# Attention gate's second block and the forget gate's 16 columns as two blocks of 264 columns

## Chip, cores and metric

The kernel runs on one core of one Trainium2 chip. The metric is the device time of one execution in microseconds, as the median of several. Its engines are TensorE (PE, with its weight loads as PEld), VectorE (DVE), ScalarE (ACT), GpSimd (POOL) and SyncE (SP), each with an instruction order of its own; DMA transfers are issued from SP's queue (loads) and POOL's (stores).

## What is computed

Two layers of a trunk over 512 tokens of 2048 features, in float32. Each layer normalizes the tokens, multiplies them with one wide matrix, cuts the result by columns, and runs two groups of heads on it:

```python
def hybrid_layer(x, w_in, w_out, g_pre, g_post, w_alpha, b_alpha, g_gla, g_att, rel_bias):
    h = rmsnorm(x, g_pre)
    z = h @ w_in
    gq, gk, gv, gg, ga, aq, ak, av, ag = split_columns(z)
    log_a = jax.nn.log_sigmoid((ga @ w_alpha + b_alpha).astype(jnp.float32)) / GLA_TAU
    o_gla = gla_chunk_causal(gq, gk, gv, log_a)
    o_gla = rmsnorm(o_gla, g_gla) * jax.nn.silu(gg)
    o_att = chunk_band_attention(aq, ak, av, rel_bias)
    o_att = rmsnorm(o_att, g_att) * jax.nn.silu(ag)
    y = jnp.concatenate([o_gla, o_att], axis=-1) @ w_out
    return x + rmsnorm(y, g_post)
```

The change is about two of the pieces of `z`: `ag`, 1024 columns, the gate of the attention heads, and `ga`, only 16 columns, the low-rank input of the forget gate `log_a`.

## The kernel before

**Precision.** A float32 operand is kept as a high part, which TensorE's fp32r format holds, and a low part, the rest. A product is three matmuls: high x high, high x low, low x high. For a block of weights the high part `wh` is a cast on ACT (L201) and the low part `wl` a subtraction on DVE (L210); for sums of tokens the same pair stands at L105 and L106.

**Blocks.** The columns of `w_in` come in blocks of 512. Each block is loaded in eight chunks of 256 features (128 partitions x 2 x 512, 512 KB). A list `stream` of jobs, one for each chunk, fixes the order of all loads, casts and subtractions; `ahead` runs up to five loads, four casts and three subtractions in front of the matmuls. The rings that the jobs use have 5 buffers for `raw` (the loaded chunk), 4 for `wh`, 3 for `wl`.

**Two kinds of products.** Most blocks are taken in pairs by `fast_gemm` (L324 on), which computes four quarter products with seven multiplications, as Strassen does; its matmuls are at L388 (512 columns) and L378 (256 columns). It needs sums and differences S1 to S4 of the token operands. The two blocks AG0 and AG1 of the attention gate are plain products in `std_gemm`, with the matmul at L310: for each chunk and each tile of 128 tokens 2 x 3 matmuls of 512 columns, into one PSUM tile for each of the token tiles. `lag` holds back the last chunks, which are then taken token tile by token tile, so that the tiles are complete one after another. `gate` (L730 on) puts a SiLU over a finished tile (L733) and stores it.

**What else is going on in these stages.** `pump` takes steps of side tasks between the matmuls, at a `rate` for each group of them. In layer 0, AG0 runs on the raw tokens; meanwhile `first_operands` makes the normalized token operands `a`, `g`, `sa` (multiplications L659 and splits L105 and L106 on DVE and ACT), which AG1 needs, chunk by chunk. In layer 1 the gate blocks run twice, for the first and the second half of the tokens, with a transposition of the normalized tokens (L521) and its evictions (L532) in between. `token_sums` makes S1 to S4 in both layers (L570 to L579 on DVE, then L105 and L106), in a few slots g4 to g7 and g10 that are used again and again, and POOL's queue stores them to memory (`S<-g`). So the cast that fills a slot anew waits for the store before. Then the pair AV of `fast_gemm` begins.

**The forget gate.** `load_forget_gate` loads the 16 columns of `w_ga` apart from the blocks, splits them with six small casts and subtractions, and lays them out as 96 columns (three groups of high and low part). The task `forget_gate` multiplies all token operands with them: 64 matmuls a layer at L752, with weights of 96 columns over 256 tokens, spread among AG1's matmuls. A copy (L759), a cast (L760) and a subtraction (L761) make the transposed `gaT` from it, which is stored for later use.

**The order** in each engine's queue is that of a scheduler, which moves instructions that do not depend on each other; rates, lags and rings decide what it can move.

## Time and profile before

| What | Value |
|---|---|
| Median of 3 runs (lowest, highest) | 1615.99 us (1614.28, 1617.05) |
| Span of the profiled execution | 1613.3 us |
| PE matmuls in the profile | 8938 |
| Layer 0's gate blocks: AG1 from, AV from | 50.65 us, 101.98 us |
| Layer 1's gate blocks: from, AV from | 804.93 us, 903.91 us |
| Granted TensorE clock | 1.00 in the stages of the gate blocks |

The profile is one execution, and its span can be compared with spans only; the runs' median is 2.7 us above it. The time of a matmul in the lists of single instructions runs from its start to its modelled end and overlaps that of the next one; its price in a stream is the distance from start to start, which the chain of work gives as length by count. The same holds in part for DVE, where an instruction of 0.68 us can be followed by the next one after 0.60.

### The profile page before, as it was taken

To read this page: it belongs to the slowest core of one execution; us is meant where nothing else is said; L and a number is where in the kernel's file an instruction comes from. 1 tells how busy PE (TensorE), PEld (TensorE's weight loads), DVE (VectorE), ACT (ScalarE), POOL (GpSimd) and SP (SyncE) were. 2 spreads that over 40 slices of the span, in tenths; PEclk is the share of its full clock that TensorE was granted. 3 is DMA by queue.
4 is the path that set the end of the run, shared out by engine and by line. 5 is a ranking of instruction groups with operands and counts; after the bars stand their busy time and mean duration, and the time that the engine had idled before them with its cause. 6 is when DMAs were issued, how large, how long until landed. Compare 5 with 4: busy or idle time off the path is not lost.

```text
span 1613.3 us, 24483 instructions
## 1 busy us (share of the span) xinstructions
PE 1600.6 (99%) x8938; PEld 1372.9 (85%) x8938; DVE 1271.7 (79%) x1646; ACT 919.5 (57%) x1509; POOL 127.5 (8%) x192
## 2 busy tenths in 40 slices
PE   9999999999999999999999999999999999999997
PEld 7888999998888778888888889999988887788886
DVE  5977777678677878998998677776786878689887
ACT  7544445657555546565796444455675545566654
POOL 0120000010000010100122000000100100101001
PEclk9999999999999999999999999999999999999999
DMA  9797686785868768689779786857858687686986
GB/s 371 258 371 271 238 304 206 230 308 168 286 213 282 261 221 313 227 309 377 270 267 369 312 312 222 306 193 260 299 198 292 209 301 254 221 307 228 342 302 190
DMA packets 133928, 438.17 MB, mean 272 GB/s; under 512 B 14404, under 2 KB 27204, under 8 KB 133776
## 3 DMA queue, kind: packets, MB, share of 16 engines
q1 hardware_dynamic: 117072, 375.99, 67.2%
q0 software_dynamic: 16160, 59.53, 10.0%
q8 instruction: 71, 1.16, 0.3%
q10 hardware_dynamic: 576, 1.08, 0.2%
q14 instruction: 49, 0.40, 0.1%
HBM read 377.02 MB, written 61.62 MB: 272 GB/s over the span
## 4 chain that ended last, share of the span: by engine, by line
PE 95%; DVE 2%; DMA 1%; ACT 1%; issue 1%; DVEq 0%; SPq 0%; ACTq 0%
PE mm L388 54%; PE mm L378 19%; PE mm L310 10%; PE ax L945 2%; PE ax L388 2%; PE ax L1131 1%; PE ax L928 1%; PE ax L752 1%; PE ax L1103 1%; PE ax L908 1%; PE ax L907 1%; PE ax L906 1%; DVE wl L210 1%; DMA bias<-in_rel_dram 0%; PE ax L1223 0%
## 5 line engine op out<-in xcount | busy, mean ns | idle before, releaser
L388 PE MATMUL mm<-wh,sa 128*128 128x512 f32 x1600 | 517.7, 394 | 0.6 <-ACT wh L201 0.5
L201 ACT CAST wh<-H 128x1024 fp32r<-128x1024 f32 x256 | 268.5, 1051 | 213.9 <-PE mm L388 94.0
L210 DVE TENSOR_TENSOR wl<-H,wh 128x1024 fp32r<-128x1024 f32 x256 | 311.6, 1219 | 94.3 <-PE mm L388 33.0
L388 PEld LDWEIGHTS mm<-wh,sa 128*128 128x128 f32 x1600 | 299.4, 188 | 72.8 <-issue 8.8
L201 ACT CAST wh<-raw 128x1024 fp32r<-128x1024 f32 (+1 forms) x233 | 244.0, 1051 | 197.1 <-PE mm L388 91.2
L210 DVE TENSOR_TENSOR wl<-raw,wh 128x1024 fp32r<-128x1024 f32 (+1 forms) x233 | 282.0, 1213 | 58.1 <-PE mm L388 25.7
L388 PE MATMUL mm<-wl,sa 128*128 128x512 f32 x800 | 312.6, 391 | 0.0
L378 PE MATMUL mm<-sa,wh 128*128 128x256 f32 x1280 | 237.4, 285 | 0.0
L388 PE MATMUL mm<-wh,a 128*128 128x512 f32 x640 | 211.5, 394 | 0.0
L378 PEld LDWEIGHTS mm<-sa,wh 128*128 128x128 f32 x1280 | 200.3, 191 | 0.3
L378 PE MATMUL mm<-sa,wl 128*128 128x256 f32 x640 | 180.9, 283 | 0.0
L388 PEld LDWEIGHTS mm<-wl,sa 128*128 128x128 f32 x800 | 150.3, 188 | 30.0 <-DVE wl L210 0.4
L195 DVE TENSOR_TENSOR H<-H,raw 128x1024 f32<-128x1024 f32 x144 | 174.6, 1217 | 1.0
L388 PEld LDWEIGHTS mm<-wh,a 128*128 128x128 f32 x640 | 119.5, 188 | 24.9
L388 PE MATMUL mm<-wl,a 128*128 128x512 f32 x320 | 125.6, 393 | 0.0
L378 PEld LDWEIGHTS mm<-sa,wl 128*128 128x128 f32 x640 | 122.5, 191 | 0.0
L430 POOL TENSOR_TENSOR sm<-sm,mhalf 128x2 f32<-128x2 f32 (+2 forms) x40 | 51.4, 1285 | 761.2 <-DVE sm L955 456.3
L197 DVE TENSOR_TENSOR raw<-H,raw 128x1024 f32<-128x1024 f32 x56 | 68.5, 1222 | 51.8 <-DMA raw<-in_w_dram 51.4
L388 PE MATMUL mm<-wh,g 128*128 128x512 f32 x320 | 101.5, 391 | 0.0
L378 PE MATMUL mm<-a,wh 128*128 128x256 f32 x512 | 95.4, 285 | 0.0
L340 ACT COPY ev<-mm 128x512 f32<-128x512 f32 x104 | 60.9, 585 | 60.5 <-PE mm L388 43.8
L216 DVE TENSOR_TENSOR H<-H,raw 128x1024 f32<-128x1024 f32 x48 | 58.7, 1223 | 35.3 <-DMA raw<-in_w_dram 35.0
(250 smaller groups left out, 2323.6 us busy)
## 6 DMA issues: line engine op xcount, KB each, us to landing
raw<-in_w_dram SPq DMA_DIRECT2D x311, 512.0 KB, 5.1
sa<-S SPq DMA_DIRECT2D x184, 512.0 KB, 4.5
H<-in_w_dram SPq DMA_DIRECT2D x64, 512.0 KB, 5.2
sa<-A SPq DMA_DIRECT2D x48, 512.0 KB, 5.8
S<-g POOLq DMA_DIRECT2D x32, 512.0 KB, 9.1
sa<-oS SPq DMA_DIRECT2D x32, 512.0 KB, 5.2
oS<-g POOLq DMA_DIRECT2D x16, 512.0 KB, 4.4
oS<-sa POOLq DMA_DIRECT2D x16, 512.0 KB, 5.7
```

Of the source, the lines that this page charges most:

```text
L195: nc.vector.tensor_tensor(out=h, in0=h, in1=r, op=ALU.add)
L197: nc.vector.tensor_tensor(out=r, in0=h, in1=r, op=ALU.subtract)
L201: last_cast[0] = nc.scalar.copy(self.wh[:, z, :], src[:, z, :]).ins
L210: last_low[0] = nc.vector.tensor_tensor(out=self.wl[:, z, :], in0=self.src[:, z, :], in1=self.wh[:, z, :].bitcast(F32), op=ALU.subtract).ins
L216: nc.vector.tensor_tensor(out=h, in0=h, in1=self.src, op=ALU.add)
L310: nc.tensor.matmul(pss[o], a(part, kk, o) if callable(a) else a[:, part, t], rhs[:, kk, :], start=(i == 0 and kk == 0 and m == 0), stop=(i ...
L340: last_copy[0] = nc.scalar.copy(e, src[t]).ins
L378: nc.tensor.matmul(dst, lhs[:, kk, f], a[:, part, tok], start=(fresh and kk == 0 and m == 0 and ft % 2 == 0), stop=(c == 3 and kk == 1 and ...
L388: last_mm[0] = nc.tensor.matmul(out_ps[t], a[:, part, tok], rhs[:, kk, :], start=(fresh and kk == 0 and m == 0), stop=(c == 3 and kk == 1 ...
L430: nc.gpsimd.tensor_tensor(out=out_r, in0=v, in1=mhalf[:, : v.shape[-1]], op=ALU.pow)
L752: nc.tensor.matmul(ps[0:96, half * 256 : (half + 1) * 256], wga[kt // 10][:, kt % 10, :], op[:, i, (kt % 2) * 256 : (kt % 2 + 1) * 256], s ...
L945: nc.tensor.matmul(o, self.pt[i][:, j * P : (j + 1) * P], av[hd // 4, j // 2][:, j % 2, (hd % 4) * P : (hd % 4 + 1) * P], start=(j == 0), ...
```

## The change

AG1 keeps only its first 264 columns. A third block AG2 takes the remaining 248 columns of the attention gate and the 16 columns `ga`, so that it is 264 wide as well. Both come from a new array `w_ag`, with chunks of 128 x 2 x 264 (264 KB). Jobs, tiles of PSUM and the SiLU use the first 264 (or 248) columns of their tiles. In layer 0 the rate of the side tasks goes from 1.8 to 1.0 and the lag from 2 to 1 in AG1, 2 in AG2; in layer 1 the rate is 1.3 in AG0 and 0.7 in AG1 and AG2.

```diff
+        def cut(self, tile_):
+            if self.b0 not in (AG1, AG2):
+                return tile_
+            return tile_.rearrange("p k n -> p (k n)")[:, : 2 * N1].rearrange("p (k n) -> p k n", k=2)
...
+            if blk in (AG1, AG2):
+                last_load[0] = nc.sync.dma_start(flat(tile_)[:, : 2 * N1], w_ag[self.l, int(blk == AG2), c]).ins
+                return self.cut(tile_)
...
-            stream += [Job(l, "std", c, b) for half in range(2) for b in (AG0, AG1) for c in CO]
+            stream += [Job(l, "std", c, b) for half in range(2) for b in (AG0, AG1, AG2) for c in CO]
...
-        pss = {o: ps_mm.tile([P, W], F32, tag="mm", name=nm("mm")) for o in outs}
+        wide = W if blk == AG0 else N1
+        pss = {o: ps_mm.tile([P, W], F32, tag="mm", name=nm("mm"))[:, :wide] for o in outs}
...
-            std_gemm(l, AG1, range(NT), CO, operand_in, gate_evac(1), rate=1.8, lag=2)
+            std_gemm(l, AG1, range(NT), CO, operand_in, gate_evac(1), rate=1.0, lag=1)
+            std_gemm(l, AG2, range(NT), CO, operand_in, gate_evac(2), rate=1.0, lag=2)
...
-                        l, b, (2 * half, 2 * half + 1), CO, operand_in, gate_evac(q), rate=1.3, lag=2 * half * q,
+                        l, b, (2 * half, 2 * half + 1), CO, operand_in, gate_evac(q), rate=0.7 if q else 1.3,
+                        lag=2 * half * (q // 2),
```

When a tile of AG2 is complete, DVE copies its last 16 columns three times into a slot `ga` of zeros (new line 752). The forget gate's own load, casts, subtractions and 64 matmuls a layer are gone; four transposes a layer (new line 764) turn `ga` into the same 96 rows. The task starts after the gate blocks and runs in AV, which now pumps at a rate of 0.5.

```diff
         def gate_evac(q):
             def f(o, ps):
                 gate(q, o, ps)
+                if q == 2:
+                    if not ga:
+                        ga.append(slot("g16", [NT, 3, 2, GA]))
+                        nc.gpsimd.memset(ga[0][:, :, :, 1, :], 0.0)
+                    for g in range(3):
+                        nc.vector.tensor_copy(ga[0][:, o, g, 0, :], ps[:, N1 - GA :])
             return f
...
-            for half in range(2):
-                for k in range(2 * KT):
-                    kt, i = k // 2, k % 2
-                    op = A[kt // 8, half, (kt // 2) % 4]
-                    nc.tensor.matmul(
-                        ps[0:96, half * 256 : (half + 1) * 256], wga[kt // 10][:, kt % 10, :],
-                        op[:, i, (kt % 2) * 256 : (kt % 2 + 1) * 256],
-                        start=(k == 0), stop=(k == 2 * KT - 1),
-                    )
-                    if k % 8 == 7:
-                        yield
+            for t in range(NT):
+                nc.tensor.transpose(
+                    ps[0:96, t * P : (t + 1) * P], ga[0][:, t].rearrange("p g c r -> p (g c r)"), ident
+                )
...
         drain()
+        tasks.append(forget_gate())
...
-        fast_gemm(l, PAIRS[0], av_consume)
+        fast_gemm(l, PAIRS[0], av_consume, rate=0.5)
```

Lines of the changed kernel have new numbers: L310 becomes L322, L201 L212, L210 L221, L106 L109, L105 L108, L659 L671, L733 L739, L388 L400.

How this moves instructions shows at three places. In layer 0, PE in the last third of AG1 before: the forget gate's matmuls (L752, weights in g16 and g17) stand among those of AG1.

```order
L310 MATMUL mm_104_621<-wl_139_810,a122_121_692 128x512
L310 MATMUL mm_104_621<-wh_130_750,a122_121_692 128x512
L752 MATMUL ax_162_952<-a110_60_342,g16_132_754 96x256 x4
L752 MATMUL ax_162_952<-a111_109_634,g16_132_754 96x256 x4
L310 MATMUL mm_105_622<-wh_130_750,a122_121_692 128x512
L310 MATMUL mm_105_622<-wl_139_810,a122_121_692 128x512
```

The same place in the changed kernel, the end of AG1 (a123 is the last operand but one; mm_104 and mm_105 are AG1's tiles, mm_170 is AG2's first):

```order
L322 MATMUL mm_107_624<-wl_144_864,sa_134_780 128x264
L322 MATMUL mm_104_621<-wh_138_816,a123_130_763 128x264 x2
L322 MATMUL mm_104_621<-wl_144_864,a123_130_763 128x264
L322 MATMUL mm_104_621<-wh_138_816,a123_130_763 128x264
L322 MATMUL mm_105_622<-wh_138_816,a123_130_763 128x264 x2
L322 MATMUL mm_105_622<-wl_144_864,a123_130_763 128x264
L322 MATMUL mm_105_622<-wh_138_816,a123_130_763 128x264
L322 MATMUL mm_170_1022<-wh_145_866,a110_60_342 128x264
L322 MATMUL mm_170_1022<-wl_150_909,a110_60_342 128x264
```

AG2's first chunks, whose operands are long there, follow ahead of AG1's last matmuls on sa_134. DVE makes those operands; here are the low parts of a123 and of the last operand (sa_128) before:

```order
L210 TENSOR_TENSOR wl_148_870<-raw_131_752,wh_140_812 128x1024
L579 TENSOR_TENSOR H_59_339<-H_59_339,g14_67_383 128x512
L106 TENSOR_TENSOR g7_142_817<-g14_67_383,g7_142_817 128x512
L106 TENSOR_TENSOR a123_127_733<-H_123_707,a123_127_733 128x512
L573 TENSOR_TENSOR g2_119_684<-H_114_666,g2_119_684 128x512
L106 TENSOR_TENSOR sa_128_738<-g3_125_719,sa_128_738 128x512
L210 TENSOR_TENSOR wl_157_930<-raw_141_814,wh_149_872 128x1024
```

And in the changed kernel (the last operand is sa_134):

```order
L671 SCALAR_TENSOR_TENSOR g3_128_749<-g13_76_432,gcol_172,bias_3_178 128x256 x2
L221 TENSOR_TENSOR wl_150_909<-raw_139_818,wh_145_866 128x528
L585 TENSOR_TENSOR g2_119_696<-H_117_684,g2_119_696 128x512
L109 TENSOR_TENSOR a123_130_763<-H_126_737,a123_130_763 128x512
L591 TENSOR_TENSOR H_59_339<-H_59_339,g14_67_383 128x512
L109 TENSOR_TENSOR g7_142_843<-g14_67_383,g7_142_843 128x512
L221 TENSOR_TENSOR wl_156_954<-raw_146_868,wh_151_911 128x528
L109 TENSOR_TENSOR sa_134_780<-g3_128_749,sa_134_780 128x512
```

The order around them is much the same, but the low parts of the weights between them are half as large and belong already to AG2. The third place is ACT in the second half of layer 1, among the casts of AG1's weights; DMASW names a wait for a store of POOL's queue. Before:

```order
L201 CAST wh_1705_8726<-raw_1699_8692 128x1024 [waits DMAHW6_49,PE_49]
L733 ACTIVATE t2_1707_8730<-mm_1666_8507 128x512
L105 CAST g5_1696_8672<-H_1551_7950 128x512 [waits DMASW6_49,DVE_49]
L105 CAST g2_1700_8695<-g3_1623_8291 128x512 [waits DVE_49]
L201 CAST wh_1713_8763<-raw_1706_8728 128x1024 [waits DMAHW7_49,PE_49]
L105 CAST g10_1701_8700<-g3_1623_8291 128x512 [waits DMASW2_49]
L201 CAST wh_1716_8797<-raw_1714_8765 128x1024 [waits DMAHW0_49,PE_49]
L105 CAST g7_1708_8734<-H_1556_7971 128x512 [waits DMASW1_49,DVE_49]
L105 CAST g6_1703_8714<-g3_1623_8291 128x512 [waits DMASW3_49]
L201 CAST wh_1719_8839<-raw_1717_8799 128x1024 [waits DMAHW2_49,PE_49]
```

The changed kernel:

```order
L212 CAST wh_1761_9064<-raw_1755_9030 128x528 [waits DMAHW4_49,PE_49]
L108 CAST g2_1756_9033<-g3_1653_8485 128x512 [waits DVE_49]
L739 ACTIVATE t2_1763_9068<-mm_1722_8845 128x512
L212 CAST wh_1768_9092<-raw_1762_9066 128x528 [waits DMAHW5_49,PE_49]
L108 CAST g10_1757_9038<-g3_1653_8485 128x512 [waits DMASW7_49]
L212 CAST wh_1771_9110<-raw_1769_9094 128x528 [waits DMAHW6_49,PE_49]
L108 CAST g7_1764_9072<-H_1586_8165 128x512 [waits DMASW0_49,DVE_49]
L108 CAST g6_1759_9052<-g3_1653_8485 128x512 [waits DMASW1_49]
L212 CAST wh_1774_9128<-raw_1772_9112 128x528 [waits DMAHW0_49,PE_49]
```

The sums' casts keep their places between the casts of weights, one block of which is now a chunk of 264 columns: as many blocks apart, but shorter ones.

53 lines of the change are left out of this document (27 added, 26 removed).

## The prediction

> **What bounds the kernel now.** I read the page first, for the engines and the chain of work that ended last.
>
> ```profile
> PE 1600.6 (99%) x8938; PEld 1372.9 (85%) x8938; DVE 1271.7 (79%) x1646; ACT 919.5 (57%) x1509; POOL 127.5 (8%) x192
> PE 95%; DVE 2%; DMA 1%; ACT 1%; issue 1%; DVEq 0%; SPq 0%; ACTq 0%
> ```
>
> TensorE (PE) is busy for 1600.6 of 1613.3 us, so it idles 12.7 us in the whole run. A change is worth what it takes from PE's own work, less any new time in which PE waits. Next I read the chain in order of time, for the price of one matmul in each of its shapes.
>
> ```profile
> 34.48 44.90 PE mm L310 x198
> 81.69 1.89 PE ax L752 x16
> 101.98 76.26 PE mm L388 x336
> 178.24 64.55 PE mm L378 x538
> 836.71 1.75 PE ax L521 x16
> ```
>
> The start, the length and the count of each piece stand there. L310 and L388 are matmuls over 512 columns: 44.90/198 = 0.2268 and 76.26/336 = 0.2270 us each. L378 runs over 256 columns: 64.55/538 = 0.1200. The forget gate's L752 (96-wide weights, 256 columns) takes 1.89/16 = 0.118, and a transpose (L521) 1.75/16 = 0.109. The idle time of PE before L310, from the view of that line, shows whether anything now holds back the attention gate blocks:
>
> ```profile
> its engine sat idle before it (us, times) until:
>   ACT wh L201: 1.4, 2
>   DVE a L106: 0.6, 1
> ```
>
> Almost nothing does: 2.0 us in three waits. Last, how much room the helpers have in the stages that the change touches. The columns are stretch, length, busy time (with count) of PE, PEld, DVE, ACT, POOL, then granted clock, DMA share and GB/s:
>
> ```profile
> 34.00:102.00 68.00, 68.00 (x334) 57.48 (x333) 63.63 (x110) 40.48 (x66) 14.73 (x27) 1.00 0.86 310
> 102.00:178.00 76.00, 76.00 (x336) 62.77 (x336) 56.30 (x52) 34.41 (x37) 1.63 (x3) 1.00 0.82 303
> 817.00:860.00 43.00, 42.85 (x210) 35.88 (x210) 36.05 (x55) 34.39 (x64) 8.19 (x14) 1.00 0.89 299
> 860.00:904.00 44.00, 44.00 (x222) 37.27 (x221) 33.65 (x40) 23.74 (x32) 9.96 (x19) 1.00 1.02 404
> ```
>
> Layer 0's gate stage (34 to 102) has DVE at 94%, and the second half of layer 1's (860 to 904) has the DMA engines full. PE is the bound, with a helper close behind it in both.
>
> **PE's own work.** Before, AG1 is 192 matmuls of 512 columns in each layer: 384 x 0.227 = 87.2 us. After, AG1 and AG2 are 768 matmuls of 264 columns. No row has this width. From 256 to 512 columns the time grows by 0.107 us, 0.42 ns a column, so 264 columns cost 0.120 + 8 x 0.00042 = 0.123 us. The nearest rows bound it by 0.120 and 0.227; it lies 8 columns from the first of them, so I keep 0.120 to 0.126 for the range (the gain would be gone at 0.132). 768 x 0.123 = 94.5 us, +7.3 (+5.0 to +9.6). Removed are 128 x 0.118 = 15.1 us. Added are 8 transposes, 8 x 0.109 = 0.9 us. Net: +7.3 - 15.1 + 0.9 = **-6.9 us**, about 3.45 in each layer (bounds -9.2 to -4.6). The Trainium skill (TensorE: Matmul & The Clock Gate, "Back-to-back issue gap") gives N/2.4 + 2.5 ns for an isolated matmul, that is 112.5 ns at 264 columns and 215.8 at 512; by it AG1 would grow by only 768 x 0.1125 - 384 x 0.2158 = +3.5 us, and the net would be -10.7. The rows above have 227 and 120 ns, some 11 ns above that formula, so the trace's fixed cost for each matmul decides here, and it is just this that speaks against cutting a block in two.
>
> **Layer 0: can DVE follow?** Here DVE makes AG1's operands while PE already runs AG1, and a chunk of AG1 now lasts 24 x 0.123 = 2.95 us in place of 5.45 plus its share of the forget gate.
>
> ```profile
> 50.65 0.39 PE L310 MATMUL mm<-wh,a 128*128 128x512 f32 x1
> ```
>
> That is AG1's first matmul. DVE, from AG1's first operand on:
>
> ```profile
> 43.01 2.35 DVE L210 TENSOR_TENSOR wl<-raw,wh 128x1024 fp32r<-128x1024 f32 x2
> 45.28 0.68 DVE L106 TENSOR_TENSOR a<-H,a 128x512 fp32r<-128x512 f32 x1
> ...
> 57.56 0.87 DVE L659 SCALAR_TENSOR_TENSOR g<-g,gcol,bias 128x256 f32<-128x256 f32 x2
> 58.35 0.68 DVE L106 TENSOR_TENSOR a<-H,a 128x512 fp32r<-128x512 f32 x1
> 58.95 0.87 DVE L659 SCALAR_TENSOR_TENSOR H<-g,gcol,bias 128x256 f32<-128x256 f32 x2
> ```
>
> From start to start, a pair of L659 costs 0.79 us, a 512-wide subtract 0.60, a 1024-wide one 1.14, so a 528-wide one about 0.62. By the order of the changed kernel the last operand but one (a123, its low part) stands behind nine of the 528-wide, twelve pairs and 23 of the 512-wide, counted from AG1's first low half at 43.01 + 1.14 = 44.15 (the second of the x2 row): 44.15 + 5.6 + 9.5 + 13.9 = 73.1 us. PE asks for it at its 177th matmul of 264 columns: 50.65 + 176 x 0.123 = 72.3. So PE waits 0.8 us even if DVE never stops. The last operand (sa_134) is ready at 73.1 + 2.4 = 75.5 and asked for at 50.65 + 205 x 0.123 + 0.8 = 76.7, because AG2's first chunks are pulled ahead of it: covered. I add 0.7 for DVE's own waits and take **+1.5 us**. Bounds: 0, and 3.45 (DVE's 4.4 idle us of this stage can't be used at all, and the stage keeps its 68 us).
>
> DVE's other changes here about cancel: eight 1024-wide lows become sixteen 528-wide ones (16 x 0.62 - 8 x 1.14 = +0.8), twelve copies of 16 columns are added, 0.15 each by the nearest row below (+1.8), the forget gate's six subtracts go (1.29), and its copy and subtract at the end move into AV, where DVE has 20 of 76 us free. ACT loses the six casts and, with them, a wait of 2.0 us for the load:
>
> ```profile
> 55.75 1.29 DVE L106 TENSOR_TENSOR g<-t,g 128x160 fp32r<-128x160 f32 x6
> ...
> 822.95 0.15 DVE L448 TENSOR_REDUCE sm<-sm 128x1 f32<-128x5 f32 x1
> ```
>
> ```profile
> L105 ACT CAST g<-t 128x160 fp32r<-128x160 f32 x3 | 0.8, 322 | 2.0 <-DMA t<-in_w_ga_dram 2.0
> ```
>
> The copies hold AG2's PSUM tiles, and AV's first product needs two of them. Those two are complete 24 matmuls (3.0 us) or more before AG2's end, and a SiLU (0.6) with three copies (0.5) takes 1.1: I cost it at nothing, and at up to 1.1 if those 3.0 us of AG2 do not cover it. Four more SiLUs and stores in a layer fall on ACT (40 of 68 us busy) and POOL: nothing. The transposes' chain (copy, cast, subtract, store) ends in a store that is read much later: nothing.
>
> **Layer 1: the store chain.** In the second half ACT's casts of the weights stand in one order with the casts of the token sums, and each of these writes into a slot whose last content must first have been stored:
>
> ```profile
> 861.23 0.62 ACT L105 CAST g<-g 128x512 fp32r<-128x512 f32 x1 [0.90 <-DVE g L576]
> ...
> 869.67 1.14 ACT L105 CAST g<-g 128x512 fp32r<-128x512 f32 x2 [1.18 <-DMA S<-g]
> ...
> 882.14 0.62 ACT L105 CAST g<-g 128x512 fp32r<-128x512 f32 x1 [2.25 <-DMA S<-g]
> ```
>
> ```profile
> DMA packets 5221, 17.76 MB, mean 404 GB/s; under 512 B 577, under 2 KB 939, under 8 KB 5218
> ...
> S<-g POOLq DMA_DIRECT2D x15, 512.0 KB, 10.9
> raw<-in_w_dram SPq DMA_DIRECT2D x13, 512.0 KB, 11.1
> ```
>
> Slot g7 is filled at 861.23 and free again at 869.67, 8.4 us later; g10, the second of the pair at 869.67, is filled from 870.2 and free at 882.14, 12.0 later. In the changed order slot g7 goes round twice between the casts of AG0's sixth and AG1's seventh block. From PE's start of the one to its start of the other lie three blocks of 12 x 0.227 = 2.72 us and six of 12 x 0.123 = 1.48: 17.1 us. ACT runs at most three blocks ahead (four wh buffers), 8.2 us in AG0, of which one cast takes 1.0; behind the last wait two sums' casts and one of weights still follow, 1.8. So 17.1 + 7.2 - 1.8 = 22.5 us are there for two landings, which need 8.4 + 12.0 = 20.4 (no wait) to 2 x 12.0 = 24.0 (1.5 us). The same stores now share full DMA engines with the loads in fewer microseconds, so I take the upper one, and 0.2 for the shorter lead in the first half, where ACT is busy 34.4 of 43 us: **+1.7 us**, bounds 0 and 3.5 (all of this layer's gain).
>
> **The sum.** -6.9 + 1.5 + 1.7 = -3.7. The profiled execution took 1613.3 us, so the changed one should take 1609.6; the median of the runs, 1615.99, stands 2.7 above it, which gives 1612.3. Beyond the two stages the order of instructions is the same on every engine, and PE idles nowhere for long, so what is saved there stays saved.
>
> **The rivals.** About 0.2% (3.2 us) is what a measurement of this kernel can tell from no change.
>
> - *Full cover*, chance 0.20: neither term appears, -6.9, 1609.1 us. For it: PE's idle time before L310 is only 2.0 us now, and AG2's matmuls are there to fill in. Against it: the 0.8 us above is short without any mishap.
> - *The forecast*, 0.42: -2.0 to -5.7, 1610.3 to 1614.0, likeliest 1612.3.
> - *The helpers become the bound*, 0.25: DVE in layer 0 (3.4 us) and the store chain in layer 1 (3.5) take all that PE gives: 0, 1616.0 us. For it: DVE's 94% and the DMA share of 1.02. Against it: in layer 0 DVE's idle time lies behind 82 us, past the operands.
> - *Short rows starve the weight stream*, 0.13, slower. Rows of 2112 bytes take the place of rows of 4096: with one packet a row, 2048 for the sixteen blocks of the second half of layer 1, for 1024 before. In the full stretch 5221 packets take 1.02 x 16 x 44 us, 137 ns each. If a packet's price does not fall with its size, 1024 x 137/16 = 8.8 us of DMA time are added where there is none free, and PE waits for weights: -6.9 + 1.5 + 8.8 = +3.4, 1619.4 us. It is slower than before from an added 5.4 us on, that is from (8.8 + 5.4) x 16/2048 = 111 ns a packet; in proportion to bytes (3402 on the mean) it would be 85 ns and nothing is added. The Trainium skill (DMA: Bandwidth & Descriptors, "Measured (HBM→SBUF, 128 partitions, SWDGE, issued from GpSimd)") asks for transfers of 1 MiB or more for three quarters of the peak, which speaks against cutting loads of 512 KB to 264. By that rule this rival gains; the trace has 404 GB/s with loads and stores of 512 KB, so it has not borne the rule out.
>
> That the change doesn't do what it says I see no room for: the order has 768 matmuls of 264 columns, 8 transposes, and no matmul of the forget gate's weights.
>
> **How the numbers follow.** Faster by over 0.2% means under 1612.8: full cover (0.20) and some three quarters of the forecast (0.31), 0.51. Slower means over 1619.2: most of the last rival, 0.12. Between them 0.37. For 8 in 10 the range runs from just below full cover, 1608.6, to 1618.6; the last rival and the far end of PE's bounds are left out. The likeliest case's own range is 1610.3 to 1614.0.
>
> **What would show it.** Right: L322 at 0.123 us a matmul in the chain; gate stages shorter by about 2 us each; one or two waits of PE for DVE operands near 72 us and for ACT casts of weights in the second half of layer 1; no change in length elsewhere. Wrong: 264 columns at 0.130 or more (the gain is gone: 768 x 7 ns = 5.4 us); PE idle for over 5 us in one gate stage, then the releaser (DVE's operand, ACT's cast behind a store, or a raw load) names the rival; a landing of raw well over 11 us names the last one.

## The result, and the profile after

The changed kernel is slower: 1628.01 us, the median of 6 runs (1623.09 to 1629.59), beside 1616.57 (1614.28 to 1618.54) for the kernel before on the same chip. The ratio is 1.0067 [1.0057, 1.0077]. The prediction said 1612.3, faster, with 1618.6 as the upper end. The profiled execution took 1629.59 us, the slowest of the six; its span is 1627.8.

The page of the changed kernel, engines and chain of the work that ended last:

```profile
PE 1603.4 (99%) x9202; PEld 1386.6 (85%) x9202; DVE 1275.0 (78%) x1682; ACT 920.8 (57%) x1529; POOL 133.5 (8%) x202
PE 86%; DMA 4%; issue 4%; DVE 4%; ACT 1%; POOL 1%; SPq 0%; DVEq 0%; POOLq 0%; ACTq 0%
```

PE's own share of the chain fell from 95% to 86%, and PE now idles 24.4 us (1627.8 - 1603.4) in place of 12.7. Its busy time even rose by 2.8 us, although its work shrank; the clock below is most of the reason. The table has the stages of the traces in us. AV of layer 0 and the stages behind it are counted from the start of their first matmul; only layer 1's gates end, and its AV begins, with the start of the last gate matmul. (The values given for the kernel before have AV 0.16 us later in layer 0, from the chain, and 0.22 later in layer 1, from AV's first matmul.)

| Kernel | L0: AV from | L0: AV | AV's end to L1's gates | L1: gates | L1: AV | to PE's end |
|---|---|---|---|---|---|---|
| before | 101.82 | 76.26 | 626.85 | 98.76 | 76.74 | 622.76 |
| after | 104.45 | 76.74 | 627.60 | 109.07 | 77.94 | 622.29 |

Layer 0's gate stage ends 2.6 us later, where 3.45 earlier was predicted before any wait; layer 1's is 10.3 us longer, where 3.45 shorter was. The other stages change by 1.2 us at most. So both losses are in the two stages that the change touches.

**Layer 0.** The gate matmuls stand at L322 now, SiLU at L739, splits of token sums at L108 and L109, casts of weights at L212, low parts at L221. PE's instructions of 72 to 78 us that waited (start, length, what, idle time before and its releaser):

```profile
72.50 0.39 PE L322 MATMUL mm<-wh,sa 128*128 128x264 f32 x1 [0.20 <-ACT sa L108]
73.67 0.51 PE L322 MATMUL mm<-wh,a 128*128 128x264 f32 x2 [0.42 <-DVE a L109]
77.51 0.59 PE L322 MATMUL mm<-wh,a 128*128 128x264 f32 x1 [2.61 <-ACT t L739]
```

The second is the predicted wait for a low part of DVE, near the predicted place; the first is for a high part, which ACT makes. Both together are 0.6 us. The third, 2.61 us, was not foreseen: it is AG2's first matmul, and what releases it is not an operand but AG1's SiLU. `mm` has four PSUM buffers, AG1 holds all four to its end, and AG2's first tile is AG1's first. ACT's instructions there:

```profile
76.03 0.63 ACT L890 ACTIVATE bias<-bias 128x512 f32<-128x512 f32 x1 [2.53 <-DMA bias<-in_rel_dram]
76.57 0.60 ACT L108 CAST g<-H 128x512 fp32r<-128x512 f32 x1
77.08 0.66 ACT L739 ACTIVATE t<-mm 128x264 f32<-128x264 f32 x2
```

ACT itself stood still for 2.53 us, at an activation that waits for the load of a bias table and that the order has ahead of the SiLU. PE's busy time in the stretches behind (columns as in the prediction):

```profile
76.00:78.00 2.00, 0.49 (x2) 0.49 (x3) 1.64 (x5) 1.97 (x5) 0.25 (x1) 0.60 0.90 275
78.00:80.00 2.00, 2.00 (x11) 2.00 (x11) 2.00 (x4) 0.25 (x1) 1.86 (x4) 0.50 0.72 194
80.00:82.00 2.00, 2.00 (x11) 2.00 (x10) 0.30 (x1) 0.00 (x0) 0.57 (x2) 0.50 0.95 371
82.00:84.00 2.00, 2.00 (x14) 2.00 (x13) 0.23 (x1) 0.60 (x2) 0.00 (x0) 0.70 1.04 424
84.00:104.00 20.00, 20.00 (x167) 20.00 (x166) 16.02 (x29) 11.79 (x22) 7.10 (x14) 1.00 0.98 379
```

The granted clock is 0.50 until behind 82 us: eleven matmuls in 2 us in place of sixteen. So the wait costs more than its own length, and the slow matmuls count as busy time. The means of 0.60 and 0.70 come from where the windows are cut: the trace has one stretch of 6.83 us at 0.50, from 76.39 to 83.22.

**Layer 1.** What PE waited for there (engine and line, us in total, times, longest), and the three longest waits:

```profile
PE mm L322 <- ACT wh L212: 6.9, 3, 3.2
PE mm L322 <- DVE wl L221: 0.8, 2, 0.5
```

```profile
860.59 0.73 PE L322 MATMUL mm<-wh,g 128*128 128x512 f32 x2 [1.58 <-ACT wh L212]
899.23 0.81 PE L322 MATMUL mm<-wh,g 128*128 128x264 f32 x2 [2.14 <-ACT wh L212]
908.61 0.51 PE L322 MATMUL mm<-wh,sa 128*128 128x264 f32 x2 [3.17 <-ACT wh L212]
```

PE waits for ACT's casts of weights. What did ACT wait for? Its casts ahead of these places, and the casts of token sums for which the prediction feared:

```profile
859.49 1.04 ACT L212 CAST wh<-raw 128x1024 fp32r<-128x1024 f32 x1 [2.75 <-DMA raw<-in_w_dram]
883.82 0.62 ACT L108 CAST g<-g 128x512 fp32r<-128x512 f32 x1 [0.72 <-DMA S<-g]
887.67 0.62 ACT L108 CAST g<-g 128x512 fp32r<-128x512 f32 x1 [0.15 <-DMA S<-g]
892.02 0.62 ACT L108 CAST g<-g 128x512 fp32r<-128x512 f32 x1 [0.21 <-DMA S<-g]
898.54 0.63 ACT L212 CAST wh<-raw 128x528 fp32r<-128x528 f32 x1 [1.03 <-DMA raw<-in_w_ag_dram]
900.47 0.63 ACT L212 CAST wh<-raw 128x528 fp32r<-128x528 f32 x1 [1.29 <-DMA raw<-in_w_ag_dram]
907.93 0.63 ACT L212 CAST wh<-raw 128x528 fp32r<-128x528 f32 x1 [4.92 <-DMA raw<-in_w_ag_dram]
```

At the end of each of PE's three long waits, or shortly behind it, the clock is low again, each time for 3.41 us:

```profile
861.45:864.86 3.41, 3.01 (x7) 2.43 (x8) 3.19 (x9) 2.84 (x5) 1.08 (x2) 0.50 0.65 211
899.00:902.41 3.41, 3.18 (x13) 2.94 (x14) 1.42 (x2) 0.84 (x3) 0.00 (x0) 0.50 1.03 417
909.24:912.65 3.41, 3.29 (x15) 3.29 (x16) 1.48 (x3) 1.44 (x3) 0.00 (x0) 0.50 1.08 393
```

The store chain is there but small, 1.1 us in three waits. The long waits are for the loads of the chunks themselves. The loads of 862 to 918 us (KB each, median us from issue to landing):

```profile
raw<-in_w_ag_dram SPq DMA_DIRECT2D x16, 264.0 KB, 8.7
S<-g POOLq DMA_DIRECT2D x16, 512.0 KB, 10.3
```

Five `raw` buffers are as many jobs of lookahead. A job of AG1 or AG2 is 12 matmuls of 0.1214 us here, 1.46 us, so that five are 7.3 us, less than the 8.7 that a load takes. Before, five jobs of 2.72 were 13.6, more than 11.1. My theory was therefore: a PSUM tile in layer 0 and the lookahead of the raw ring in layer 1, each with a low clock behind the wait. The rivals: the rows of 2112 bytes starve the loads; what a gate stage saves is lost to transfers behind it anyway; the 264-column matmuls are dearer.

### The profile page after: what moved, and what is told of

It is laid out like the page before. It is cut to its first block, busy times and chain, and to the rows that moved or that the text cites. A ratio compares the mean times of both kernels' runs of the same rounds, so it can differ in the third digit from the quotient of the medians.

```text
span 1627.8 us, 25201 instructions
## 1 busy us (share of the span) xinstructions
PE 1603.4 (99%) x9202; PEld 1386.6 (85%) x9202; DVE 1275.0 (78%) x1682; ACT 920.8 (57%) x1529; POOL 133.5 (8%) x202
## 4 chain that ended last, share of the span: by engine, by line
PE 86%; DMA 4%; issue 4%; DVE 4%; ACT 1%; POOL 1%; SPq 0%; DVEq 0%; POOLq 0%; ACTq 0%
PE mm L400 52%; PE mm L390 18%; PE mm L322 5%; PE ax L954 2%; PE ax L400 2%; DMA raw<-in_w_dram 1%; DVE wl L221 1%; PE ax L1140 1%; PE ax L937 1%; PE ax L1112 1%; DMA raw<-in_w_ag_dram 1%; DMA S<-g 1%; PE ax L917 1%; PE ax L916 1%; PE ax L915 1%
## 5 line engine op out<-in xcount | busy, mean ns | idle before, releaser
L400 PE MATMUL mm<-wh,sa 128*128 128x512 f32 x1600 | 517.7, 394 | 1.4 <-DMA sa<-S 0.9
L212 ACT CAST wh<-H 128x1024 fp32r<-128x1024 f32 x256 | 268.1, 1051 | 208.5 <-PE mm L400 92.0
L221 DVE TENSOR_TENSOR wl<-H,wh 128x1024 fp32r<-128x1024 f32 x256 | 311.5, 1220 | 84.8 <-PE mm L400 33.3
L212 ACT CAST wh<-raw 128x1024 fp32r<-128x1024 f32 (+2 forms) x257 | 249.7, 975 | 216.5 <-PE mm L400 83.8
L400 PEld LDWEIGHTS mm<-wh,sa 128*128 128x128 f32 x1600 | 299.5, 188 | 73.8 <-issue 9.9
L221 DVE TENSOR_TENSOR wl<-raw,wh 128x1024 fp32r<-128x1024 f32 (+2 forms) x257 | 286.7, 1119 | 87.3 <-PE mm L400 27.4
L400 PE MATMUL mm<-wl,sa 128*128 128x512 f32 x800 | 312.6, 391 | 0.0
L400 PE MATMUL mm<-wh,a 128*128 128x512 f32 x640 | 211.4, 394 | 0.0
L400 PEld LDWEIGHTS mm<-wl,sa 128*128 128x128 f32 x800 | 150.3, 188 | 30.1 <-DVE wl L221 0.4
L400 PEld LDWEIGHTS mm<-wh,a 128*128 128x128 f32 x640 | 119.4, 188 | 24.8
L400 PE MATMUL mm<-wl,a 128*128 128x512 f32 x320 | 125.7, 393 | 0.0
L400 PE MATMUL mm<-wh,g 128*128 128x512 f32 x320 | 101.4, 391 | 0.0
```

The costliest lines, as they stand in the source:

```text
L212: last_cast[0] = nc.scalar.copy(self.wh[:, z, :], src[:, z, :]).ins
L221: last_low[0] = nc.vector.tensor_tensor(out=self.wl[:, z, :], in0=self.src[:, z, :], in1=self.wh[:, z, :].bitcast(F32), op=ALU.subtract).ins
L400: last_mm[0] = nc.tensor.matmul(out_ps[t], a[:, part, tok], rhs[:, kk, :], start=(fresh and kk == 0 and m == 0), stop=(c == 3 and kk == 1 ...
```

## The experiments

Each kernel is compared with the kernel before, run beside it. Lines of the table that follow the experiments are read as in the one above.

**AG2's PSUM tiles from another pool.** In layer 0 AG2 takes the four tiles of `ax`, so that nothing holds it behind AG1's SiLU.

```diff
-        pss = {o: ps_mm.tile([P, W], F32, tag="mm", name=nm("mm"))[:, :wide] for o in outs}
+        if l == 0 and blk == AG2:
+            pss = {o: aux()[:, :wide] for o in outs}
+        else:
+            pss = {o: ps_mm.tile([P, W], F32, tag="mm", name=nm("mm"))[:, :wide] for o in outs}
```

> Theory (waits and the clock after them): in layer 0 AG2's first tile of PSUM is AG1's first, which a SiLU has to empty, and that SiLU stands on ACT behind the bias load (2.53 us). PE waits 2.61 us and then runs at a granted clock of 0.5 for some 6 us. With AG2's tiles in the other PSUM pool this wait has no cause: no wait of PE on ACT near 77 us, granted clock 1.00 through the stage, AV of layer 0 begins at about 98.7 instead of 104.2, the run is some 5.5 us shorter than the changed kernel's (about 1622). Rival (DVE makes AG1's operands too late, as predicted): at most 1 us shorter, since only 0.6 us of DVE waits stand there and they stay.

1625.15 us, 1.0054 [1.0042, 1.0067]. AV starts at 97.65 us, 6.8 us earlier than in the changed kernel, but takes 79.07 in place of 76.74, so that only some 4.5 us are left at its end. The median is 2.9 us below the changed kernel's, where 5.5 was expected.

**The wait filled with work.** 24 matmuls of 256 columns that nobody reads stand between AG1 and AG2 in layer 0; nothing else is changed.

```diff
+            if l == 0 and blk == AG1 and i == n - 1 and o == 1:
+                ps_f = aux()
+                for z in range(24):
+                    nc.tensor.matmul(ps_f[:, :256], A[0, 0, 0][:, 0, 0:P], A[0, 0, 0][:, 0, 0:256], ...)
```

> The changed kernel with 24 idle matmuls of 256 columns (24 x 0.12 = 2.9 us, their result is read by nobody) between AG1's last matmul on a123 and AG2's first matmul in layer 0, just where PE waited 2.61 us for the SiLU. Theory (the low clock follows from PE standing still): the SiLU is as late as before, but PE is busy meanwhile, the granted clock stays at 1.00 after 77 us, and AV of layer 0 begins 2.9 us earlier than in the changed kernel, at 101.5, though PE has 2.9 us more to do. Rival (the clock drops for another reason, or the drop costs nothing since DVE is the limit there): AV begins at 104.4 or later.

1622.22 us, 1.0039 [1.0025, 1.0052]. The chain of work of this kernel (start, length, what, count):

```profile
74.47 2.88 PE ax L331 x24
77.35 24.32 PE mm L322 x200
101.67 1.62 PE mm L405 x7
```

The same 200 matmuls that took 27.10 us take 24.32, 0.1216 each, and AV starts at 101.50 in place of 104.45. Nothing waits less; PE is only kept busy. So 2.8 us of layer 0's loss (27.10 - 24.32) were the low clock behind the wait; the rest of the 2.95 is an AG2 that starts 0.16 us earlier.

**One layer alone.** Only layer 0 is split, or only layer 1; the other one is as before.

```diff
+SPLIT = (True, False)   # the second kernel: (False, True)
...
-            if blk in (AG1, AG2):
+            if blk in (AG1, AG2) and SPLIT[self.l]:
```

> Only layer 0 has the two narrow blocks; layer 1 is as before. Theory (the time is lost within the two gate stages): layer 0 costs 2 to 3 us, AV of layer 0 begins at about 104, layer 1's gate stage has its old length of 99 us, the median is 1619 to 1620. Rival (it is lost outside, for example to the forget gate's transposes in AV or to later stages): clearly over 1620, with the shift growing past layer 0's AV.

> Only layer 1 has the two narrow blocks. Theory: layer 0 as before (AV at 102.0), layer 1's gate stage about 10 us longer than before, through waits of PE for the weights (their casts wait for loads) and the low clock after each; median 1625 to 1628. Rival (layer 1's loss was a consequence of layer 0's later start): near 1617 or below.

Layer 0 alone: 1615.37, 0.9998 [0.9989, 1.0006]; layer 1 alone: 1621.53, 1.0038 [1.0025, 1.005], its gate stage 104.98 us. So layer 1 bears the larger part. Both lost less than expected (1619 to 1620, and 1625 to 1628). The two don't add up to the whole, because layer 0 was luckier alone: its wait for the SiLU was 1.70 us and the clock stayed at 1.00 behind it, where 2.61 us cost the clock. Length alone does not decide this: in layer 1 of the changed kernel a wait of 1.58 us was followed by the low clock, while one of 2.08 us (the kernel with doubled stores below) and one of 2.43 (the joined kernel below) were followed by 1.00. Layer 1's stage, the same program in four kernels, took 105.0, 105.5, 105.9 and 109.1 us, the last in the changed kernel's profiled run.

**A longer lookahead.** One job for both narrow blocks of a chunk, with one load of 528 KB, raw buffers of 528 x 2 columns, and seven scratch buffers in place of eight to make room. Five jobs are 14.6 us then. A second kernel loads the same buffer in two transfers of 264 KB, with the rows of the changed kernel.

```diff
-            stream += [Job(l, "std", c, b) for half in range(2) for b in (AG0, AG1, AG2) for c in CO]
+            stream += [Job(l, "std", c, b) for half in range(2) for b in (AG0, AG1) for c in CO]
...
-                last_load[0] = nc.sync.dma_start(flat(tile_)[:, : 2 * N1], w_ag[self.l, int(blk == AG2), c]).ins
+                last_load[0] = nc.sync.dma_start(tile_, w_ag[self.l, c].rearrange("p (k n) -> p k n", k=2)).ins
```

> The same 264-wide matmuls, but each chunk of 256 features is one job for both narrow blocks: one load of 528 KB, one cast and one low part of 1056 columns, then the matmuls of both blocks on it, in two PSUM tiles (the second from the other pool). One of eight small scratch buffers is given up for the space. Theory (short jobs halve the time that the rings look ahead, and the PSUM tiles are handed on too early): blocks last 5.8 us in layer 0 and 2.9 in layer 1, longer than before, no wait over 1 us, the predicted saving of PE's work comes out, 1610 to 1613. Rival (DVE in layer 0 and the full DMA engines in layer 1 are the limit whatever the job's size): layer 0's stage keeps 68 us and layer 1's waits stay, 1617 or more.

> The joined jobs again (one cast and one low part for both narrow blocks of a chunk), but each chunk comes in two loads of 264 KB with rows of 2112 bytes, as in the changed kernel. Theory (the jobs' length, and with it how far the five raw buffers reach ahead, decides): layer 1's gate stage takes 95 to 96 us as with joined loads, median within 2 us of theirs (1620). Rival (short rows slow the weight stream): layer 1's stage is 3 us longer or more.

1620.12, 1.0035 [1.0022, 1.0047], and 1623.57, 1.0046 [1.0029, 1.0063]. Layer 1's gate stage is 95.23 and 95.34 us: 3.5 below the kernel before, the whole of what PE's own work gives. The size of the transfers and their rows made no difference to it. The medians lie 3.5 us apart all the same, where 2 at most were expected. That stands in layer 0's AV, which takes 84.13 us with half loads and 81.04 with joined ones: PE's longest wait there is 3.94 us, with 3.41 us of low clock behind it, beside 2.43 us without. With half loads a cast there waits 1.28 us for a load of H; whether the size of the gate blocks' loads has to do with that is not shown. And both kernels lose 3 to 4 us in each of the long stages without gates, which no theory of mine said.

**Less and more to transfer.** Half of every S store, each half loaded twice, on top of AG2's tiles in `ax`; and, the other way, the kernel before with eight of layer 0's sixteen S stores doubled (4.2 MB more).

```diff
-            nc.gpsimd.dma_start(dst[name, c], flat(op))
+            nc.gpsimd.dma_start(dst[name, c][:, :W], flat(op)[:, :W])
```

```diff
+            if dst is sa_d[0] and c > 1:
+                nc.gpsimd.dma_start(extra[name, c], flat(op))
```

> The changed kernel with AG2's tiles in the other PSUM pool in layer 0, as before, and with only half of each token sum stored and loaded twice over, so that products with sums are computed from other numbers; every engine does the same work, and 4.2 MB of stores (10 us of full DMA engines) are missing in each gate stage. Theory (DMA engines that are full until after AV's start eat the gain in layer 0, and make AG1's and AG2's weights late in layer 1): AV of layer 0 begins at 97.7 and takes 76.7 us without waits, layer 1's gate stage takes 95 to 97 us in place of 106, the run is about 1609. Rival (jobs of 264 columns are too short for ACT, DVE and the rings whatever the DMA does): layer 1's stage stays over 103 us.

> The kernel before with eight of the 16 stores of sums in layer 0 made twice, to two places, of which each later load takes one half: 4.2 MB more stores in the stage, 10 us of full DMA engines, the same work on PE, DVE and ACT. Theory (the DMA engines' backlog at the change from the gate blocks to AV has no room to spare in the kernel before, so less PE work ahead of it only turns into waits): the engines stay full until 125 us or later, PE waits in AG1's end or AV, and layer 0's AV ends 4 to 10 us later (before: 178.1). Rival (DVE's order paces that place): AV ends within 1 us of 178.1.

With half the stores: 1619.01, 1.0018 [1.0009, 1.0028]. In layer 1 the same sixteen loads land sooner, and the five narrow buffers suffice but for 2.5 us of waits; the stage takes 99.4 us, between what the theory (95 to 97) and the rival (over 103) expected:

```profile
raw<-in_w_ag_dram SPq DMA_DIRECT2D x16, 264.0 KB, 5.8
```

With more stores: 1619.63, 1.0019 [1.0009, 1.0028]. Here nothing is split; AV of layer 0 starts where it did, at 101.70, and takes 79.01 us:

```profile
112.11 0.73 PE L393 MATMUL mm<-wh,a 128*128 128x512 f32 x2 [2.08 <-ACT wh L206]
```

So 4.2 MB more to store make layer 0's AV 2.75 us longer: the cast that PE waits for stands behind loads of H. AV ends 2.6 us later than before (180.71 for 178.08), less than the 4 to 10 of the theory and more than the 1 of the rival. Halving the stores helps AV little: it takes 78.85 us for 79.07. PE's waits at its start shrank from 1.7 to 0.2 us, but others came later (two for `sa<-S`, 0.5 us), and the order of DVE's instructions at AV's start is another in that kernel.

**Two that missed.** Four stores of 512 KB more in the kernel before, meant for about 84 us (1616.14, 1.0007 [0.9997, 1.0016]). Nobody reads what they store, so nothing holds them at their place, and the trace has them issued from 41.7 us on, long before AV:

```profile
41.73 2.35 POOL L317 DMA_DIRECT2D ex<-a  x4 [9.66 <-DVE a L107]
```

There the DMA engines had room (share 0.47 from 40 to 50 us in the kernel before, 0.77 here), so this run says nothing on AV's start. And AG1 and AG2 ahead of AG0 in layer 1, so that the narrow jobs come before the DMA engines are full:

```diff
+                nc.gpsimd.dma_start(extra[o], flat(A[0, 0, 0]))
```

```diff
-                for q, b in enumerate((AG0, AG1, AG2)):
+                for q, b in ((1, AG1), (2, AG2), (0, AG0)):
```

> The kernel before with four more stores of 512 KB into unused memory, issued from POOL's queue in AG1's sixth chunk of layer 0 (about 84 us); nothing else differs. Theory (from 84 us to some 118 the DMA engines are full, and what they have to move decides when AV's first loads are there): 2.1 MB at 415 GB/s are 5.1 us more, the engines stay full until about 123, AV of layer 0 gets waits of PE for casts behind H loads and grows from 76.3 to 78 us or more. Rival (AV's start in the kernels with less PE work waits for DVE or ACT): AV keeps 76.3 us.

> The changed kernel with AG2's tiles in the other PSUM pool in layer 0, and in layer 1 the two narrow blocks ahead of AG0 in each half, so that the short jobs run while few stores of sums are under way, and the 512-wide jobs, whose five raw buffers hold 13.6 us of matmuls, where the DMA engines are full. Theory (short jobs are starved only where the DMA engines are full): layer 1's gate stage takes 97 us or less in place of 106, without a wait of over 1 us, and the median is 1612 to 1616. Rival (the narrow jobs are starved by their own length, anywhere): waits for their loads appear at the start of the stage and it stays over 103 us.

The swap took 1630.21 us, 1.0088 [1.0073, 1.0103], its stage 113.9: at the start PE waits for operands instead (1.57 and 2.02 us), at the end AG0's loads land after 13.1, which the 13.6 us of its five buffers hardly cover. (AV's first matmul stands 109.7 us behind the stage's start there, ahead of AG0's last.) That theory fell; the rival had the length, but not the waits at the start, which are not for loads.

**Layer 0 alone, with AG2's tiles from `ax`.** The two edits together, layer 1 as before.

> Only layer 0 is split into two blocks of 264 columns, with AG2's PSUM tiles from the aux pool so that its first matmul does not wait for AG1's SiLU; layer 1 is the kernel before. My accounting (a wait for a PSUM tile and the low clock behind it, layer 1's ring of raw buffers, and a hand-over to the first FM blocks at which the DMA engines are full): AV starts at about 97.7 us as with both layers split and aux tiles, loses about 2.5 us again in AV, so that the first 256-column block stands about 1.4 us earlier than before, and layer 1's gate stage keeps its 98.8 us: about 1614.5 us, a ratio of 0.999. Rival, that nothing that layer 0 saves ever reaches the end, because the FM loads behind it are bound by the DMA engines alone: 1616 us or more, with the first 256-column block where it was.

1613.88 us (1612.03 to 1616.06), 0.9983 [0.9974, 0.9992]: this one is faster than both kernels, but than the kernel before by only 0.17%, less than the 0.2% that the prediction took as the least that can be told from no change. AV starts at 97.53, with no wait of PE in the gate stage, and gives 2.8 us back, 1.7 of them here:

```profile
108.28 0.50 PE L406 MATMUL mm<-wl,a 128*128 128x512 f32 x1 [0.96 <-DVE wl L223]
114.80 0.50 PE L406 MATMUL mm<-wl,a 128*128 128x512 f32 x1 [0.78 <-DVE wl L223]
```

What held DVE's low parts (L223) up? The cast of the first one's weights, DVE's order, and the last of the forget gate's transposes on PE:

```profile
103.26 2.00 ACT L214 CAST wh<-H 128x1024 fp32r<-128x1024 f32 x2 [0.24 <-DMA H<-in_w_dram]
103.03 1.29 DVE L111 TENSOR_TENSOR g<-g,g 128x512 fp32r<-128x512 f32 x2
106.41 0.69 DVE L799 COPY g<-ax 96x512 f32<-96x512 f32 x1 [2.10 <-PE ax L784]
107.02 1.21 DVE L223 TENSOR_TENSOR wl<-H,wh 128x1024 fp32r<-128x1024 f32 x1
106.10 0.27 PE L784 MATMUL ax<-cst,g 128*96 128x128 f32 x1
```

The cast was done by 105.3, but in DVE's order the forget gate's copy (L799) stands ahead of the low part, and it waits 2.10 us for the transpose. From there to 115.8 us DVE does not stop, and the copy and the forget gate's subtraction are 1.4 us of that. The kernel of the first experiment and the last two below have the same order there, with 1.7 to 2.5 us of idle time before the copy. So the first of these waits comes from the forget gate's chain, which the change moved into AV, and the second stands behind it in DVE's order. No run moved it elsewhere, so how much of the 2.8 us would come back is not shown.

**Where the joined kernels' gain went.** Three controls compute what the kernel before computes: seven scratch buffers; these and all buffers of the ring (`raw`, `wh`, `wl`) 1056 columns wide, of which 1024 are used; seven scratch buffers and `raw` alone widened. And a kernel with layer 0 as in the last one and layer 1 joined.

```diff
-            self.wh = rtile("wh", dtype=F32R)
+            self.wh = rtile("wh", (2 * 528,), dtype=F32R)[:, : 2 * W].rearrange("p (k n) -> p k n", k=2)
```

> The kernel before with seven in place of eight scratch buffers, as the kernels with joined jobs have it, and nothing else. Theory (the joined kernels lose 3.0 us between layer 0's AV and layer 1, and 3.7 us behind layer 1's AV, to this alone): those stretches, 626.9 and 622.8 us before, grow to about 630 and 626, the run to about 1622. Rival (the joined jobs themselves cost that time): no change from 1616.

> The kernel before with seven scratch buffers and with the ring's buffers (raw, wh, wl) 1056 columns wide in place of 1024, of which 1024 are used: nothing is computed in another way, only the tiles stand at other places and distances in SBUF. If the joined kernels' later losses come from the place or the stride of the ring's tiles, it shows them too: 629.9 us between the layers and 626.3 behind layer 1's AV, about 1622 us, 1.004. If they come from the order in which the joined jobs leave the pools and queues: as with seven scratch buffers alone, 628.3 and 623.1, about 1617.3 us, 1.0008.

> As the kernel before with seven scratch buffers, and of the ring's buffers only the five raw ones are 1056 columns wide: wh and wl move by 640 bytes in each partition and keep their distance of 4096 bytes from one to the next. If it is the place that made the 512-column matmul 0.2308 us instead of 0.2268 and the 256-column one 0.1190 instead of 0.1200, the two prices are shown here again and the time is about 1626 us. If it is the distance between the tiles (4224 bytes): 0.227 and 0.120, and 1617.3 us.

> Layer 0 as in the kernel with only layer 0 split (blocks of 264, AG2's PSUM tiles from the aux pool), layer 1 with both narrow blocks in one job for each chunk (528 KB in one load), seven scratch buffers as in the first kernel with joined jobs. If layer 1's loss came from the short lookahead of its ring of raw buffers and what its gate stage wins is kept: gate stage 95.3 us in place of 98.8, the first 256-column block of layer 0 at 176.6, and the part behind layer 1's AV as long as before, 622.7 us: about 1611.8 us, a ratio of 0.997. Rival, that joined jobs in layer 1 bring about the later losses seen there (626.3 us behind layer 1's AV): about 1615.5 us, 0.9995, with the gate stage at 95.3 all the same.

Scratch buffers: 1617.35, 1.0008 [0.9998, 1.0018]. Wider ring: 1627.65, 1.0067 [1.0054, 1.0081]. `raw` alone: 1626.28, 1.0064 [1.0049, 1.008]. Nothing waits in the wider ring's stretch below; the matmuls themselves are dearer:

```profile
912.61 77.55 PE mm L391 x336
990.15 64.04 PE mm L381 x538
```

77.55/336 = 0.2308 us for 512 columns, where the kernel before has 0.2270, and 0.1190 for 256, where it has 0.1200. That moving `wh` and `wl` by 640 bytes does most of it (AV of layer 1 is 77.37 us, with seven buffers alone 76.38, with the wider ring 77.78) points to the place of the operands in SBUF, more than to the distance between them. The prices there are 0.2296 and 0.1197, so that of 256 columns hardly moves, other than expected. Which address rule is behind it is open.

The joined kernel for layer 1 took 1618.37 us, 1.0012 [1.0003, 1.002], more than either expected value. Beside the control with the same ring it is 9.3 us faster (1627.65 - 1618.37), both layers together. In layer 1, stage by stage: gates 95.17 for 99.76, AV 77.88 for 77.78, the rest 625.68 for 625.72. What PE waits for in its gate stage:

```profile
PE mm L330 <- DVE wl L225: 0.2, 1, 0.2
```

So with enough lookahead layer 1's gain is made and kept; the wider ring's dearer matmuls had hidden it.

**The lookahead without a wider ring.** AG1 and AG2 take their chunks in turn from one raw buffer of 512 columns; the 16 forget columns stand in SBUF from the start, and a second small cast and subtraction puts them in place.

```diff
+            if k == "std" and self.shared():
+                self.raw = shared[0]
...
+            return ((slice(0, W - N1), self.src, slice(N1, W)), (slice(W - N1, N1), ga_w, slice(None)))
```

> Layer 0 split as in the kernel with only layer 0 split. Layer 1 split too, but AG1 and AG2 take their chunks in turn and share one load of 512 KB of the 512 columns in one raw buffer; the 16 forget columns stand in 1 KB of SBUF that is loaded once, and a second small cast and subtract puts them beside the last 248. So the five raw buffers look ahead 5 x 2.9 = 14.6 us over landings of 9 to 10, and the ring's tiles keep their 1024 columns. Seven scratch buffers make room for the 1 KB. If the short lookahead was layer 1's loss and the wider ring the joined kernels': gate stage of layer 1 at 95.5 us, 512-column matmuls at 0.227, 622.5 to 623.1 behind layer 1's AV, about 1611.5 us, a ratio of 0.997. Rival, that the sixteen small casts and subtracts for each half, or casts for two narrow blocks a chunk, hold PE up: gate stage at 98 to 99 us and 1614.5 us.

1613.98 us (1612.38 to 1616.37), 0.999 [0.9981, 0.9999]: below both kernels, by 0.1% below the one before, but no better than layer 0 alone. PE's price is right again, and a load holds up only one cast, by 0.6 us; but the stage takes 97.38 us, between the 95.5 of the theory and the 98 to 99 of the rival. In its first half PE waits in seven places, for casts and low parts above all (1.0 us counted before the matmuls alone, 2.7 with the waits of their weight loads), which is the rival's reason, and behind the stage AV waits for S to come back from memory:

```profile
940.18 0.93 PE L451 MATMUL mm<-wh,sa 128*128 128x512 f32 x3 [0.60 <-DMA sa<-S]
951.74 0.47 PE L451 MATMUL mm<-wh,sa 128*128 128x512 f32 x1 [0.43 <-DMA sa<-S]
```

| Kernel | L0: AV from | L0: AV | AV's end to L1's gates | L1: gates | L1: AV | to PE's end |
|---|---|---|---|---|---|---|
| AG2's tiles in `ax` | 97.65 | 79.07 | 628.02 | 105.92 | 77.17 | 622.55 |
| layer 0 alone, tiles in `ax` | 97.53 | 79.06 | 628.62 | 98.76 | 76.49 | 623.57 |
| both joined (528 KB) | 97.94 | 81.04 | 629.85 | 95.23 | 77.95 | 626.47 |
| before, wider ring | 103.61 | 77.41 | 631.43 | 99.76 | 77.78 | 625.72 |
| layer 0 `ax`, layer 1 joined | 98.14 | 79.97 | 630.11 | 95.17 | 77.88 | 625.68 |
| layer 0 `ax`, shared raw | 97.19 | 79.06 | 627.34 | 97.38 | 78.10 | 622.88 |

## Why the prediction was wrong, point by point

- **PE's own work, -6.9: right.** The chain of the changed kernel has the price in one row:

```profile
83.97 20.64 PE mm L322 x170
```

  20.64/170 = 0.1214 us a matmul, 0.123 predicted. With it the term is even -8.1. Where no wait is left (layer 1 joined), the stage is shorter by the 3.5 us that were worked out for it.
- **DVE's operands in layer 0, +1.5: right in place, too large.** 0.42 us for DVE's low part, at 73.7 us for 72.3 predicted, and 0.20 for a high part of ACT; with AG2's tiles in `ax`, none: AG2's matmuls then fill in, as the first rival had it.
- **"I cost it at nothing", the copies that hold AG2's PSUM: the failed step in layer 0.** It asked only who holds tiles ahead of AV. The same question one block earlier, who holds tiles ahead of AG2, was not asked: four buffers, all AG1's, and a SiLU behind a load. 2.61 us of waiting, and 2.8 of low clock.
- **The store chain in layer 1, +1.7: the failed step there.** It looked at the slots of S and at the four `wh` buffers, but not at the five `raw` buffers, whose lookahead in us is halved with the jobs' length. The waits for stores were 1.1 us on ACT and none of them was the one that PE waited for. In their place PE waited 7.7 us in five waits for weights; against the predicted 3.45 us less the stage lost 13.8. Of the other 6 us some 5 are the low clock: three stretches of 3.41 us at 0.50, in which PE was busy for 9.5 us at half its clock, which costs half of that. The profiled run is the dearest: the same stage took 105.0 to 105.9 us in the other three kernels.
- **"What is saved there stays saved": wrong in layer 0.** Of the 4.3 us that AV starts earlier with layer 0 mended, 1.5 are left at its end. What failed is a term that the prediction put at nothing: that the forget gate's copy and subtraction "move into AV, where DVE has 20 of 76 us free". Free time over the whole stage says nothing about the order: the copy stands ahead of a low part that PE needs and waits 2.10 us there. In the changed kernel itself, where AV starts later, AV grows by 0.5 us only. The DMA share of 0.82 over the whole of AV was no sign of room at its start either; the kernel before, read in shorter stretches, shows:

```profile
100.00:115.00 15.00, 15.00 (x68) 12.42 (x67) 12.84 (x12) 7.35 (x8) 2.18 (x4) 1.00 1.03 416
115.00:125.00 10.00, 10.00 (x46) 8.29 (x45) 7.02 (x7) 6.45 (x9) 0.00 (x0) 1.00 0.38 146
```

  The engines are full until 115 us, and more stores there did cost time (79.01 us of AV for 76.26). How much of what the mended kernels lose in AV is the forget gate's order and how much would be the DMA engines' stays open. In layer 1 the sentence holds, beside the control with the same ring.
- **The clock was taken as constant.** The kernel before showed 1.00 everywhere, so no row could price its fall; that PE hardly ever waited there was the sign that a new wait would show something new. The Trainium skill (TensorE: Matmul & The Clock Gate, "What's actually happening") has the clock at half after at least one idle window of about 3.4 us. By that none of the changed kernel's waits, 3.17 us at most, would have cost it by itself; its trace has 0.50 behind each of the four longest, down to 1.58 us. So the state is the page's, and less idle time can be enough for it. Not always: other kernels have 1.00 behind waits of 1.70, 2.08 and 2.43 us.
- **The rivals.** Short rows that starve the weights gave 1619.4, the nearest number, but not the mechanism: with 264 KB loads in two halves of a joined buffer, and the same rows, the stage is 95.34. And the packets did not keep their price. For 880 to 912 us of the changed kernel (queue, packets, MB, share of 16 engines):

```profile
q0 software_dynamic: 1970, 7.01, 54.2%
q1 hardware_dynamic: 3417, 5.97, 49.1%
```

  0.491 x 16 x 32 us/3417 = 74 ns for 1747 bytes on the loads' queue, 141 ns for 3558 on the stores': nearly in proportion to bytes. These are means over packets of several sizes; the trace's packet records have the rows of 2112 bytes apart, at 87 ns each, beside 161 for 4096 bytes on the same queue. The prediction's own bounds were 85 ns for proportion and 111 for a slower kernel. The sign "PE idle for over 5 us in one gate stage, then the releaser names the rival" was met and named a raw load, the sign of this rival; but the landing, 8.7 us, was shorter than before. None of the rivals had the mechanism: a load that is no slower and only asked for too late. The Trainium skill (DMA: Bandwidth & Descriptors, "Measured (HBM→SBUF, 128 partitions, SWDGE, issued from GpSimd)") asks for transfers of 1 MiB or more; here a cut from 528 to 264 KB changed the stage by 0.1 us.
- **Readings of the prediction that are a little off, without consequence.** The "2.0 us in three waits" before L310 count the first wait twice, for a weight load and for its matmul (1.1 and 0.2 us at 5.86 us, the start of the run; 0.6 at 817.15). The sums of 13.9 and 17.1 us come to 13.8 and 17.0.

## What to carry to other kernels

A ring's depth is a time: number of buffers times the length of a job. Whoever makes jobs shorter has to set that product against the landing time of the loads in the same stage, here 7.3 us against 8.7. When one block becomes two, every resource that was handed over once (PSUM tiles, slots, queue places) is handed over twice, and the new hand-over has to be costed like the old one. And a wait on PE is to be priced at its length plus what the clock loses behind it: here 2.6 us cost 2.8 more. Last, a side task that moves into another stage takes its place in the engines' orders there: what counts is not how much time an engine has free in that stage, but what stands behind the task's instructions while they wait.

## What the runs showed of the hardware

- A wait of PE of 2.61 us was followed by the clock at 0.50, for 6.83 us with the wait's end in it; waits of 1.58, 2.14 and 3.17 us by 3.41 us of it each; waits of 1.70, 2.08 and 2.43 us in other kernels by none. So length alone does not decide. Filling the wait of 2.61 us with idle matmuls kept the clock and gained 2.8 us though nothing was waited for less.
- The same matmuls cost more or less with unused columns in their operands' buffers, which only moves the tiles in SBUF: 0.2308 us in place of 0.2270 for 512 columns, 0.1190 in place of 0.1200 for 256 (in that control alone; the joined kernel for layer 1, with the same ring, has 0.1199), and some 10 us over this kernel (1.0067 against 1.0008). A comparison of two kernels with differently sized tiles needs a control that changes only the sizes.
- Loads in rows of 2112 bytes cost DMA time nearly in proportion to their bytes: 87 ns a packet where rows of 4096 bytes cost 161, which is 0.041 and 0.039 ns a byte.
